# Tables moved, c spread in two rounded parts, and loads reordered in a decoder layer

## The chip, the cores and the metric

The kernel runs on one core of one Trainium2 chip, as one program. The metric is device time in microseconds, the median over several executions; lower is better. Weights are packed on the host into the order in which they are read; that is not part of the time.

## The reference

One decoder layer on 256 tokens with 2048 channels in float32. A vector c makes six modulation vectors, which shift, scale and gate two sub-layers. The first mixes tokens with block attention (eight heads; with 256 tokens there is one block of keys) and with a gated delta rule (16 value heads); the second is a SwiGLU of width 5632.

```python
mod = jax.nn.silu(c) @ w_ada[l] + b_ada[l]
sh1, sc1, g1, sh2, sc2, g2 = jnp.split(mod[:, None, :], 6, axis=-1)
h = x * (1.0 + sc1) + sh1
y = token_mixer(h, w_in[l], conv_w[l], a_log[l], dt_bias[l], gdn_norm_w[l], rel_bias,
                w_proj_moba[l], w_proj_gdn[l], w_out[l])
x = layer_norm(DEEPNORM_ALPHA * x + g1 * y, ln1_g[l], ln1_b[l])
h = x * (1.0 + sc2) + sh2
y = swiglu(h, w_ffn_in[l], w_ffn_out[l])
x = layer_norm(DEEPNORM_ALPHA * x + g2 * y, ln2_g[l], ln2_b[l])
...
proj = h @ w_in          # in token_mixer: q, k, v of both mixers, z, gates
merged = jax.nn.sigmoid(gate_a) * (y_a @ w_proj_moba) + jax.nn.sigmoid(gate_b) * (y_b @ w_proj_gdn)
return merged @ w_out
```

## The kernel before

**Products.** Every weight is loaded as float32 (`raw`, 512 KB, 128 x 1024), rounded by ScalarE into `hi` (L235), and VectorE writes the rest, raw - hi, into `lo` (L236). Activations are split in the same way. A product is hi*hi + hi*lo + lo*hi, so three matmuls of the rounded type float32r. There are three shapes of loop:

- `ws_mm` (L329 to L331): the weights are the stationary operand, 128 x 128, and 256 tokens move. h, split into s0 (high) and s1 (low), ya and ybA with ybBh/ybBl (the outputs of the two mixers) are moved in this way.
- `xs_unit` (L377 to L379): 128 tokens of the activation are stationary and 512 columns (sometimes 256) of hi or lo move. z, the output projection (activations mh, ml) and the feed-forward output (ach, acl) use it.
- `ws_wide` (L336, L340), for the feed-forward input: the high and low half of h lie side by side and move as 512 columns past hi, then 256 columns past lo.

**Stages, by the time of the profile.** Up to 17 us the opening: c is spread over 128 partitions by matmuls with a row of ones (`load_c`, L152), passed through Silu into `cb`, and `warm` (L508) issues matmuls on zeros. Up to 305 us the start: 24 jobs (256 columns of w_in each; 16 for the delta mixer, 8 for attention) times four groups of four 128-row blocks of w_in. In the first group eight of the jobs run as a *ramp*, block by block, since each block of h needs its own two modulation columns first. The partial sums of 19 jobs are added up in SBUF by VectorE, five stay in PSUM (`kept`). From 305 to about 975 us come attention, the delta rule, z, gates, branch projections and the output projection, the two mixers' steps being interleaved with the weight jobs by lanes of generators (`tick`). From 975 to 1475 us the feed-forward input, then its output and the last LayerNorm.

**Modulation columns.** One column of 128 outputs is a 1 MB load (`w_ada`, into a ring of four buffers) and one VectorE multiply-and-sum over 2048 elements with `cb` (L255, the `r<-r,cb,cols` rows). In the start 40 columns are handled this way: `ada_to(n)` makes the sums up to n, `ada_goal` says how many are due at job i of group n. `ada_opening` issues the load of column n + 3 before it makes the sum of column n, so four columns are loaded or under way. In the first group `between` puts a block of x and the two packed ramp weights behind each pair of modulation loads.

**Queues.** All of these loads are issued by SyncE in program order. A load into a buffer still in use holds the queue. `run(3)` lets the loads and splits of up to three later jobs be issued ahead of a job's matmuls; the loads and sums that a job itself issues come behind its matmuls. `prep` makes four blocks of h (two ScalarE activations and a VectorE subtraction each) near the end of the group before.

**Addresses.** Tiles of the pool `perm` lie one behind the other in the order of first use, then the weights pool, then the pool of the mixers or of the feed-forward. In the compiled program before, these are the byte addresses within a partition:

| tiles | address | modulo 128 |
|---|---|---|
| x_sb, later ya, sgb, r | 4224 | 0 |
| cb, then jk (160 bytes) | 22848, 31040 | 64, 64 |
| dtb, nwc, epsc, adac, ada_half | 31200 to 31776 | small tables |
| s0, s1 (h; later the feed-forward's h, 128 bytes on) | 32032, 48672 | 32, 32 |
| sa and other small tables | from 65312 | |
| raw, hi, lo (several buffers) | 66176, 90752, 107136 | 0, 0, 0 |
| kq, v; later mh, ml | 132736 to 157312 | 0 |
| ring of modulation columns, later ma and ybA; ybBh | 165696, 182080 | 64, 64 |
| ybBl | 206656, 214848 | 64 |
| ach, acl | 124544, 169600 | 0, 0 |

All buffers of hi, of lo and all slices that are used as operands are whole multiples of 128 bytes apart, so the last column holds for each of them.

Of the kernel before, what the change touches and what calls it, by code (L numbers as in the profile page):

```python
# [10 lines left out]
F32 = mybir.dt.float32  # L11
F32R = mybir.dt.float32r
AF = mybir.ActivationFunctionType
OP = mybir.AluOpType
# [4 lines left out]
P = 128  # L19
D = 2048  # L20
S = 256
KT = D // P
# [83 lines left out]
def layer(ctx, tc, a, out):  # L106
    nc = tc.nc
    v_, s_, g_, t_, dma = nc.vector, nc.scalar, nc.gpsimd, nc.tensor, nc.sync
    sdma = nc.gpsimd

    perm = ctx.enter_context(tc.tile_pool(name="perm", bufs=1))
    wp = ctx.enter_context(tc.tile_pool(name="wp", bufs=3))
# [12 lines left out]
    def e2(nm, shape):  # L125
        return k1.tile(shape, F32, tag="e2", name=nm, bufs=2)
# [9 lines left out]
    def load_x(k0, kn):  # L136
        dma.dma_start(x_sb[:, k0:k0 + kn, :], a["xT"][:, k0:k0 + kn, :])

    cb = perm.tile([P, D], F32, name="cb")
    jk = perm.tile([P, 40], F32, name="jk")  # L140

    def load_c():
        ones = e2("ones", [1, P])
        v_.memset(ones, 1.0)
        dma.dma_start(cb[0:1, :], a["c"])
        ps = mm()
        for i in range(3):
            t_.matmul(ps, zero[:, :P], zero, start=True, stop=True)
        for i in range(4):
            ps = (pt.tile([P, 512], F32, tag="tp", name="ps_c") if i % 2 else  # L150
                  pg.tile([P, 512], F32, tag="gd", name="ps_c"))
            t_.matmul(ps, ones, cb[0:1, 512 * i:512 * i + 512], start=True, stop=True)  # L152
            s_.activation(cb[:, 512 * i:512 * i + 512], ps, AF.Silu)  # L153

    w_in = a["w_in"]
# [95 lines left out]
    def ada_sum(col, part, raw, parts):  # L251
        first, last = part == 0, part == parts - 1
        n = D // parts
        h = ada_half[:, col % 4:col % 4 + 1]
        v_.tensor_tensor_reduce(out=raw, in0=raw, in1=cb[:, n * part:n * part + n], scale=1.0,  # L255
                                scalar=cols[:, col:col + 1] if first else h, op0=OP.mult, op1=OP.add,
                                accum_out=adac[:, col:col + 1] if last else h)
# [11 lines left out]
                ada_sum(*held.pop(0), 2)  # L269
                yield 1.35  # L270

    def ada_opening(order, ahead, between):
        held, loaded = [], 0
        for n, col in enumerate(order):
            while loaded < min(n + ahead + 1, len(order)):
                raw = ring[loaded % len(ring)]
                dma.dma_start(raw, w_ada.tile(0, KT, order[loaded] * P, P, by_column=True))
                held.append(raw)
                loaded += 1
                between(loaded)  # L280
            raw = held.pop(0)
            if n == 0:
                for half in range(2):
                    ada_sum(col, half, raw[:, 1024 * half:1024 * half + 1024], 2)
            else:
                ada_sum(col, 0, raw, 1)
            yield

    turn = {"mm": 0, "all": False}

    def mm():
# [14 lines left out]
    def do(fn):  # L306
        prog.append((None, fn, 0))
# [86 lines left out]

    hTh, hTl = [aT(tag).rearrange("p (k i) -> p k i", i=S) for tag in ("s0", "s1")]
    h_ops = [[t[:, k, :] for k in range(KT)] for t in (hTh, hTl)]

    def g8(slot, nm, shape, dt=F32):
        return k1.tile(shape, dt, tag=f"g{slot}", name=nm)
# [39 lines left out]
    RAMP = [list(range(len(jobs) - KEPT, len(jobs) - 1)), [len(jobs) - 1, 0, 1, 2]]  # L439
    raws = {}  # L440

    def between(n):
        if n % 2 or n > 2 * GROUPS[0][1]:
            return
        k = n // 2 - 1
        load_x(k, 1)
        for part, some in enumerate(RAMP):
            raw = wp.tile([P, 1024], F32, tag="raw", name="raw", bufs=6)
            dma.dma_start(raw, w_in.columns(k, [jobs[i][0] for i in some], 256))
            raws[k, part] = raw.rearrange("p (k n) -> p k n", n=256)  # L450

    ada1 = ada_opening(ada_order[:2 * KT + EARLY], 3, between)
    ada_n = [0]

    def ada_to(n):
        while ada_n[0] < n:
            next(ada1)
            ada_n[0] += 1

    def ada_goal(n, i):  # L460
        ends = [2 * (k0 + kn) for k0, kn in GROUPS] + [2 * KT + EARLY]
# [11 lines left out]
    def prep(k0, kn):  # L473
        for f in range(k0, k0 + kn):
            by = dict(bias=adac[:, f:f + 1], scale=adac[:, 16 + f:17 + f])
            s_.activation(hTh[:, f, :], x_sb[:, f, :], AF.Identity, **by)
            hf = e2("hf", [P, S])
            s_.activation(hf, x_sb[:, f, :], AF.Identity, **by)
            v_.tensor_tensor(hTl[:, f, :], hf, hTh[:, f, :].bitcast(F32), op=OP.subtract)
# [19 lines left out]

    def warm():  # L500
        ps = mm()
        two = [zero.rearrange("p (a b) -> p a b", b=b)[:, :, :b // 2] for b in (2, 32)]
        for m in [zero] * 8 + [zero[:, 0:1].to_broadcast([P, 512])] * 3 + [zero[:, :S]] * 3 + two * 2 + [zero] * 4:
            n = 512 if m is zero or m.shape[-1] == 512 else S
            o = ps[:, :n]
            if len(m.shape) == 3:
                o = o.rearrange("p (a b) -> p a b", b=m.shape[2])
            tc.keep_in_program_order(t_.matmul(o, zero[:, :P], m, start=True, stop=True))  # L508

    warm()  # L510
    kept = []
# [2 lines left out]
    def ramp(k, part):  # L514
        def post(hi, lo):
            some = RAMP[part]
            if k == 0:
                for i in some:
                    stays = i - len(jobs) + KEPT
                    if stays < 0:  # L520
                        accs[i] = mm()
                        continue
                    p, tag, b = ((pt, "tp", 2), (pt, "tp", 2), (pg, "gd", 2), (pg, "gd", 2), (pm, "mk", 1))[stays]
                    accs[i] = p.tile([P, 512], F32, tag=tag, name="mm_kept", bufs=b)
                    kept.append(accs[i])
            for low in range(2):
                for n, i in enumerate(some):
                    for t in range(2):
                        o, c = accs[i][:, t * S:(t + 1) * S], slice(t * P, (t + 1) * P)
                        if low:  # L530
                            last = k == 3 and t == 1 and i < len(jobs) - KEPT
                            t_.matmul(o, lo[:, n, c], h_ops[0][k], start=False, stop=last)
                        else:
                            t_.matmul(o, hi[:, n, c], h_ops[0][k], start=(k == 0 and t == 0), stop=False)
                            t_.matmul(o, hi[:, n, c], h_ops[1][k], start=False, stop=False)
            if part and k < 3:
                for _ in range(5):
                    t_.matmul(kept[0], zero[:, :P], zero, start=False, stop=False)
            if part and k == 3:
                for i in some[1:]:  # L540
                    s_.copy(jobs[i][1], pairs_of(accs[i]))

        held_step(lambda: raws[k, part], 4, 256, post)

    def startup(n):
        k0, kn = GROUPS[n]
        more = n + 1 < len(GROUPS)
        if n == 0:
            for k in range(4):
                do(lambda k=k: (ada_to(2 * k + 2), prep(k, 1)))  # L550
                for part in range(2):
                    ramp(k, part)
        if more:
            do(lambda: load_x(*GROUPS[n + 1]))
        if n == 1:
            do(load_small)
            do(load_ba)
        for i, (c0, dst) in enumerate(jobs):
            if n == 0 and i in RAMP[0] + RAMP[1]:
                continue  # L560

            def post(hi, lo, i=i, dst=dst):
                stays = i - len(jobs) + KEPT
                if stays < 0:
                    ps = mm()
                    ws_mm(ps, h_ops, hi, lo, k0, kn, True, True)
                else:
                    ps = kept[stays]
                    ws_mm(ps, h_ops, hi, lo, k0, kn, False, not more)
                if n == 0 if stays < 0 else not more:  # L570
                    s_.copy(dst, pairs_of(ps))
                elif stays < 0:
                    v_.tensor_tensor(dst, dst, pairs_of(ps), op=OP.add)
                ada_to(ada_goal(n, i))
                if more and i == (17 if n else 16):
                    prep(*GROUPS[n + 1])
                if not more and i >= 8:
                    if i == 8:
                        bg["pre"].append(gdn_pre(0))
                    tick()  # L580
                if not more and i == len(jobs) - 1:
                    ada_to(2 * KT + EARLY)

            step(w_in, k0, kn, c0, 256, post)
# [881 lines left out]
```

## Time and profile before

| | |
|---|---|
| median of 3 runs | 1727.77 us (1727.2 to 1731.12) |
| profiled execution | 1732.76 us, span 1731.0 us |
| TensorE busy | 97% of the span |
| VectorE, ScalarE busy | 71%, 48% |
| moved by DMA | 412.72 MB, mean 238 GB/s |

A row of the page or of the timeline names the kernel's line (L329), the engine (PE is TensorE's matmuls, PEld its weight loads, DVE VectorE, ACT ScalarE, POOL GpSimd, SP SyncE's queue of loads), the operation, the tiles as out<-in, the shape and a count. The duration of one matmul in the rows (280 to 400 ns) includes its way through the array; several overlap, so the time that a row of matmuls takes is read from the distance between their starts, or from the count in a stretch of time.

### The profile page before, as it was taken

To read this page: it belongs to the slowest core of one execution; us is meant where nothing else is said; L and a number is where in the kernel's file an instruction comes from. 1 tells how busy PE (TensorE), PEld (TensorE's weight loads), DVE (VectorE), ACT (ScalarE), POOL (GpSimd) and SP (SyncE) were. 2 spreads that over 40 slices of the span, in tenths; PEclk is the share of its full clock that TensorE was granted. 3 is DMA by queue.
4 is the path that set the end of the run, shared out by engine and by line. 5 is a ranking of instruction groups with operands and counts; after the bars stand their busy time and mean duration, and the time that the engine had idled before them with its cause. 6 is when DMAs were issued, how large, how long until landed. Compare 5 with 4: busy or idle time off the path is not lost.

```text
span 1731.0 us, 28124 instructions
## 1 busy us (share of the span) xinstructions
PE 1686.1 (97%) x11117; PEld 1509.6 (87%) x11117; DVE 1225.2 (71%) x1724; ACT 835.8 (48%) x1176; POOL 34.5 (2%) x60
## 2 busy tenths in 40 slices
PE   9999999999899998999999999999999999999997
PEld 7899999789898798889988998888888888888885
DVE  7788989786985676457989787666666666555454
ACT  3544445679554753365434454444444444433341
POOL 0000000001010000000000000000000000000000
PEclk9999999999999999899999999999999999999998
DMA  9989886576685577557999468777777776766662
GB/s 384 414 328 359 308 307 221 175 218 207 200 257 179 162 226 236 181 184 244 304 356 353 154 216 259 223 227 224 225 222 232 227 222 221 238 192 188 197 193 72
DMA packets 110582, 412.72 MB, mean 238 GB/s; under 512 B 13053, under 2 KB 14605, under 8 KB 104941
## 3 DMA queue, kind: packets, MB, share of 16 engines
q1 hardware_dynamic: 107010, 400.13, 69.7%
q0 software_dynamic: 3440, 10.80, 2.3%
q8 instruction: 87, 1.43, 0.3%
q14 instruction: 45, 0.37, 0.1%
HBM read 406.59 MB, written 4.28 MB: 237 GB/s over the span
## 4 chain that ended last, share of the span: by engine, by line
PE 78%; DVE 9%; DMA 7%; issue 3%; ACT 2%; SPq 0%; POOL 0%; DVEq 0%; ACTq 0%; POOLq 0%
PE mm L336 17%; PE mm L340 9%; PE mm L377 8%; PE mm L379 8%; PE mm L378 8%; PE mm L331 7%; PE mm L329 7%; PE mm L330 7%; DVE lo L236 4%; DMA raw_a<-in_w_ada 3%; DMA raw<-in_w_in 1%; DVE r L255 1%; DMA Mb<-mbd 1%; PE mm_kept L331 1%; PE mm_kept L329 1%
## 5 line engine op out<-in xcount | busy, mean ns | idle before, releaser
L235 ACT CAST hi<-raw 128x1024 fp32r<-128x1024 f32 x552 | 577.2, 1049 | 710.5 <-PE mm L379 199.4
L236 DVE TENSOR_TENSOR lo<-raw,hi 128x1024 fp32r<-128x1024 f32 x552 | 672.1, 1223 | 318.1 <-ACT hi L235 315.4
L331 PE MATMUL mm<-s,lo 128*128 128x256 f32 x1208 | 343.7, 285 | 12.9 <-DVE lo L236 12.9
L329 PE MATMUL mm<-s,hi 128*128 128x256 f32 x1208 | 345.2, 286 | 2.4 <-ACT hi L235 2.4
L330 PE MATMUL mm<-s,hi 128*128 128x256 f32 x1208 | 342.0, 283 | 0.0
L336 PE MATMUL mm<-s,hi 128*128 128x512 f32 x1280 | 323.7, 395 | 0.0
L336 PEld LDWEIGHTS mm<-s,hi 128*128 128x128 f32 x1280 | 229.1, 188 | 43.2
L331 PEld LDWEIGHTS mm<-s,lo 128*128 128x128 f32 x1208 | 230.2, 191 | 15.7 <-DVE lo L236 15.4
L329 PEld LDWEIGHTS mm<-s,hi 128*128 128x128 f32 x1208 | 230.0, 191 | 4.8 <-ACT hi L235 2.6
L330 PEld LDWEIGHTS mm<-s,hi 128*128 128x128 f32 x1208 | 230.1, 190 | 1.6 <-issue 1.1
L340 PEld LDWEIGHTS mm<-s,lo 128*128 128x128 f32 x1280 | 172.2, 188 | 14.7
L340 PE MATMUL mm<-s,lo 128*128 128x256 f32 x1280 | 176.0, 280 | 0.0
L377 PE MATMUL mm<-hi,ach 128*128 128x512 f32 x352 | 137.1, 390 | 0.0
L378 PE MATMUL mm<-lo,ach 128*128 128x512 f32 x352 | 137.0, 389 | 0.0
L379 PE MATMUL mm<-hi,acl 128*128 128x512 f32 x352 | 137.0, 389 | 0.0
L255 DVE CUSTOM_DVE_ANT_0 raw_a<-raw_a,cb,cols 128x1024 f32<-128x1024 f32 x56 | 71.8, 1282 | 50.0 <-DMA raw_a<-in_w_ada 50.0
L255 DVE CUSTOM_DVE_ANT_0 raw_a<-raw_a,cb,ada_half 128x1024 f32<-128x1024 f32 x56 | 71.7, 1280 | 50.0 <-DMA raw_a<-in_w_ada 49.9
L255 DVE CUSTOM_DVE_ANT_0 r<-r,cb,cols 128x2048 f32<-128x2048 f32 (+1 forms) x40 | 92.5, 2321 | 4.1 <-ACT cb L153 4.1
L377 PE MATMUL mm<-hi,s 128*128 128x512 f32 x192 | 79.4, 414 | 0.0
L378 PEld LDWEIGHTS mm<-lo,ach 128*128 128x128 f32 x352 | 66.1, 188 | 13.8
L379 PEld LDWEIGHTS mm<-hi,acl 128*128 128x128 f32 x352 | 66.1, 188 | 13.7
L377 PEld LDWEIGHTS mm<-hi,ach 128*128 128x128 f32 x352 | 66.1, 188 | 13.6
(336 smaller groups left out, 2314.0 us busy)
## 6 DMA issues: line engine op xcount, KB each, us to landing
raw<-in_w_in SPq DMA_DIRECT2D x208, 512.0 KB, 4.6
raw<-in_w_ffn_in SPq DMA_DIRECT2D x176, 512.0 KB, 4.2
raw_a<-in_w_ada SPq DMA_DIRECT2D x112, 512.0 KB, 4.4
raw<-in_w_ffn_out SPq DMA_DIRECT2D x88, 512.0 KB, 4.2
r<-in_w_ada SPq DMA_DIRECT2D x40, 1024.0 KB, 8.8
raw<-in_w_proj_gdn SPq DMA_DIRECT2D x32, 512.0 KB, 4.5
raw<-in_w_out SPq DMA_DIRECT2D x32, 512.0 KB, 6.0
raw<-in_w_proj_moba SPq DMA_DIRECT2D x16, 512.0 KB, 4.6
```

Source lines behind the costliest of these rows:

```text
L235: s_.copy(hi, raw)
L236: low = v_.tensor_tensor(lo, raw, hi.bitcast(F32), op=OP.subtract)
L255: v_.tensor_tensor_reduce(out=raw, in0=raw, in1=cb[:, n * part:n * part + n], scale=1.0, scalar=cols[:, col:col + 1] if first else h, op0= ...
L329: t_.matmul(o, hi[:, i, c], ah, start=(first and i == 0 and t == 0), stop=False)
L330: t_.matmul(o, hi[:, i, c], al, start=False, stop=False)
L331: t_.matmul(o, lo[:, i, c], ah, start=False, stop=(last and i == kn - 1 and t == 1))
L336: t_.matmul(box[t].rearrange("p (u i) -> p u i", u=2), hi[:, i, t * P:(t + 1) * P], both[k0 + i], start=(first and i == 0), stop=False)
L340: t_.matmul(box[t][:, :S], lo[:, i, t * P:(t + 1) * P], both[k0 + i][:, 0, :], start=False, stop=(last and i == kn - 1))
L377: t_.matmul(box[h], xh, hi[:, i, :], start=start, stop=False)
L378: t_.matmul(box[h], xh, lo[:, i, :], start=False, stop=False)
L379: t_.matmul(box[h], xl, hi[:, i, :], start=False, stop=stop)
```

## The change

Three things are changed. `jk`, a small table, is made after s0 and s1 instead of before them, and has 56 columns instead of 40. `load_c` rounds c into a high part and takes a rest, both float32r, and adds two products in PSUM instead of one float32 product. And the modulation loads of the start are issued by a function of its own, `ada_load`, apart from the sums: in the first group only eight columns are loaded during the ramp, and then columns are loaded up to two beyond the goal of the job (three in later groups). The load of the next group's x moves from the start of a group to its job 9. The matmuls on zeros are also fewer in `warm`, and of 256 columns in the ramp.

```diff
-    jk = perm.tile([P, 40], F32, name="jk")
 
     def load_c():
-        ones = e2("ones", [1, P])
-        v_.memset(ones, 1.0)
+        ones = k1.tile([1, P], F32R, tag="e2", name="ones", bufs=2)
+        v_.memset(ones.bitcast(F32), 1.0)
         dma.dma_start(cb[0:1, :], a["c"])
         ps = mm()
         for i in range(3):
             t_.matmul(ps, zero[:, :P], zero, start=True, stop=True)
+        parts = []
+        for i in range(4):
+            if i % 2 == 0:
+                hi = wp.tile([P, 1024], F32R, tag="hi", name="c_hi", bufs=4)
+                lo = wp.tile([P, 1088], F32R, tag="lo", name="c_lo", bufs=4)
+            part = slice(512 * (i % 2), 512 * (i % 2) + 512)
+            raw = cb[0:1, 512 * i:512 * i + 512]
+            s_.copy(hi[0:1, part], raw)
+            v_.tensor_tensor(lo[0:1, part], raw, hi[0:1, part].bitcast(F32), op=OP.subtract)
+            parts.append((hi[0:1, part], lo[0:1, part]))
         for i in range(4):
...
-            t_.matmul(ps, ones, cb[0:1, 512 * i:512 * i + 512], start=True, stop=True)
+            for n in range(2):
+                t_.matmul(ps, ones, parts[i][n], start=(n == 0), stop=(n == 1))
             s_.activation(cb[:, 512 * i:512 * i + 512], ps, AF.Silu)
...
     hTh, hTl = [aT(tag).rearrange("p (k i) -> p k i", i=S) for tag in ("s0", "s1")]
     h_ops = [[t[:, k, :] for k in range(KT)] for t in (hTh, hTl)]
+    jk = perm.tile([P, 56], F32, name="jk")
...
-    ada1 = ada_opening(ada_order[:2 * KT + EARLY], 3, between)
-    ada_n = [0]
+    early = ada_order[:2 * KT + EARLY]
+    ada_n = {"load": 0, "sum": 0, "held": []}
+
+    def ada_load(n):
+        while ada_n["load"] < min(n, len(early), ada_n["sum"] + len(ring)):
+            at = ada_n["load"]
+            raw = ring[at % len(ring)]
+            dma.dma_start(raw, w_ada.tile(0, KT, early[at] * P, P, by_column=True))
+            ada_n["held"].append(raw)
+            ada_n["load"] += 1
+            if at % 2 and at < 2 * GROUPS[0][1]:
+                k = at // 2
+                load_x(k, 1)
+                for part, some in enumerate(RAMP):
+                    raw = wp.tile([P, 1024], F32, tag="raw", name="raw", bufs=6)
+                    dma.dma_start(raw, w_in.columns(k, [jobs[i][0] for i in some], 256))
+                    raws[k, part] = raw.rearrange("p (k n) -> p k n", n=256)
 
     def ada_to(n):
-        while ada_n[0] < n:
-            next(ada1)
-            ada_n[0] += 1
+        while ada_n["sum"] < n:
+            ada_load(ada_n["sum"] + 1)
+            raw, col = ada_n["held"].pop(0), early[ada_n["sum"]]
+            if ada_n["sum"] == 0:
+                for half in range(2):
+                    ada_sum(col, half, raw[:, 1024 * half:1024 * half + 1024], 2)
+            else:
+                ada_sum(col, 0, raw, 1)
+            ada_n["sum"] += 1
...
     def warm():
         ps = mm()
-        two = [zero.rearrange("p (a b) -> p a b", b=b)[:, :, :b // 2] for b in (2, 32)]
-        for m in [zero] * 8 + [zero[:, 0:1].to_broadcast([P, 512])] * 3 + [zero[:, :S]] * 3 + two * 2 + [zero] * 4:
...
+        for _ in range(14):
+            tc.keep_in_program_order(t_.matmul(ps, zero[:, :P], zero, start=True, stop=True))
...
             if part and k < 3:
-                for _ in range(5):
-                    t_.matmul(kept[0], zero[:, :P], zero, start=False, stop=False)
+                for n in range(12):
+                    at = 16 * (2 * k + n // 6)
+                    t_.matmul(kept[0][:, :S], zero[:, 384:], zero[:, at:at + S], start=False, stop=False)
...
             for k in range(4):
-                do(lambda k=k: (ada_to(2 * k + 2), prep(k, 1)))
+                do(lambda k=k: (ada_load(min(2 * k + 4, 8)), ada_to(2 * k + 2), prep(k, 1)))
                 for part in range(2):
                     ramp(k, part)
-        if more:
-            do(lambda: load_x(*GROUPS[n + 1]))
...
-                ada_to(ada_goal(n, i))
+                goal = ada_goal(n, i)
+                ada_to(goal)
+                ada_load(goal + (3 if n else 2))
+                if more and i == 9:
+                    load_x(*GROUPS[n + 1])
                 if more and i == (17 if n else 16):
                     prep(*GROUPS[n + 1])
```

More of the change, by code (lines that the diff above doesn't have):

```diff
@@ L270, in ada_sums @@
                 yield 1.35
[L272 to L287, printed above, removed]
     turn = {"mm": 0, "all": False}
@@ L440, in layer @@
     raws = {}
[L442 to L450, printed above, removed]
-    ada1 = ada_opening(ada_order[:2 * KT + EARLY], 3, between)
-    ada_n = [0]
-    def ada_to(n):
-        while ada_n[0] < n:
-            next(ada1)
-            ada_n[0] += 1
+    early = ada_order[:2 * KT + EARLY]
[14 more added lines that the diff above has]
+                    raws[k, part] = raw.rearrange("p (k n) -> p k n", n=256)
+    def ada_to(n):
+        while ada_n["sum"] < n:
[7 more added lines that the diff above has]
+            ada_n["sum"] += 1
     def ada_goal(n, i):
@@ L501, in warm @@
         ps = mm()
-        two = [zero.rearrange("p (a b) -> p a b", b=b)[:, :, :b // 2] for b in (2, 32)]
-        for m in [zero] * 8 + [zero[:, 0:1].to_broadcast([P, 512])] * 3 + [zero[:, :S]] * 3 + two * 2 + [zero] * 4:
[L504 to L508, printed above, removed]
+        for _ in range(14):
+            tc.keep_in_program_order(t_.matmul(ps, zero[:, :P], zero, start=True, stop=True))
     warm()
```

## The prediction, before the changed kernel was run

> **What bounds the kernel now.** I read the page of the profile first, then the busy time by windows, then the timeline of the places that the diff touches, and last the chain of work that ended last.
>
> ```profile
> span 1731.0 us, 28124 instructions
> PE 1686.1 (97%) x11117; PEld 1509.6 (87%) x11117; DVE 1225.2 (71%) x1724; ACT 835.8 (48%) x1176; POOL 34.5 (2%) x60
> DMA  9989886576685577557999468777777776766662
> PE 78%; DVE 9%; DMA 7%; issue 3%; ACT 2%; SPq 0%; POOL 0%; DVEq 0%; ACTq 0%; POOLq 0%
> ```
>
> TensorE is busy for 97% of the span, so nearly all time is the number of matmuls times the distance between two starts. That distance is what the change of addresses can touch. Windows that hold one kind of matmul give it (window, length, PE busy, count, granted clock, DMA share, GB/s):
>
> ```profile
> 170.00:300.00 130.00, 130.00 (x1098) 1.00 0.82 284
> 825.00:845.00 20.00, 20.00 (x179) 1.00 0.88 300
> 960.00:970.00 10.00, 10.00 (x86) 1.00 0.60 201
> 1480.00:1700.00 220.00, 220.00 (x972) 1.00 0.62 192
> ```
>
> All four run at clock 1.00 without an idle moment. The edges cut some 2.5 matmuls, so I divide by the count less 2.5. The first three are 256 columns wide: moving s with weights hi or lo, 130/1095.5 = 118.7 ns; moving ybA or ybBh with the same weights, 20/176.5 = 113.3 ns; moving hi or lo with weights mh, 10/83.5 = 119.8 ns. The fourth is 512 wide, moving hi with weights ach: 220/970 = 226.8 ns, exactly twice 113.3. So the same instruction has three paces. The table of addresses above orders them by the distance between moving and weight address, modulo 128 bytes: 64 gives 113.3; 32 gives 118.7; 0 gives 119.8 at 256 columns but 226.8 at 512. The other 512-wide kinds both stand at 32:
>
> ```profile
> 1199.74 2.02 PE L336 MATMUL mm<-s,hi 128*128 128x512 f32 x8
> 1201.60 1.10 PE L340 MATMUL mm<-s,lo 128*128 128x256 f32 x8
> 1202.54 2.02 PE L336 MATMUL mm<-s,hi 128*128 128x512 f32 x8
> 729.83 0.39 PE L378 MATMUL mm<-lo,s 128*128 128x512 f32 x1
> 732.16 0.39 PE L379 MATMUL mm<-hi,s 128*128 128x512 f32 x1
> ```
>
> In the feed-forward input, eight wide matmuls take 1201.60-1199.74 = 1.86 us, 232.5 ns each, and eight narrow ones 0.94 us, 117.5 ns. In z, ten starts lie 2.33 us apart, 233 ns each.
>
> The start has another bound:
>
> ```profile
> 17.10:96.70 79.60, 74.73 (x592) 0.98 1.00 399
> 96.70:305.30 208.60, 206.15 (x1730) 1.00 0.85 303
> 250.00:300.00 50.00, 50.00 (x424) 50.00 (x423) 49.73 (x73) 25.42 (x33) 3.11 (x5) 1.00 0.69 225
> ```
>
> The first group of w_in rows (192 ramp matmuls, 15 fillers, 384 of the other 16 jobs, which is x592) ends at 96.7 with the DMA engines full; the three other groups (3 x 24 x 24 = 1728 matmuls) end at 305.3. In the third row (PE, PEld, DVE, ACT, POOL) VectorE is at 49.73 of 50 us.
>
> **The change, part by part.**
>
> *Addresses.* jk had 160 bytes ahead of s0 and s1; now 224 bytes stand behind them. So s0 and s1 move down by 160 and everything from sa on moves up by 64. Modulo 128: s from 32 to 0; hi, lo, raw, kq, mh, ach from 0 to 64; ma0, ybA, ybB from 64 to 0; x_sb's place, which ya has later, stays at 0. The distances become: s to hi or lo, 64 instead of 32 (all of L329 to L331, L336, L340 and z's L377 to L379 with s); ya to hi, 64 instead of 0; ybA to hi stays 64; mh and ach to hi stay 0. No instruction is added.
>
> For 256 columns the new distance is the one that ybA shows, so I take 113.3. For 512 columns no row has distance 64. The bounds are 226.8 (no penalty, as at 0) and twice 119.8, 240 (the worst narrow pace, doubled). I take 226.8: it is nearest to the narrow pace that does have distance 64, doubled, and every row with both addresses at a multiple of 64 shows either no penalty or the one of distance 0. The terms:
>
> ```profile
> L336 PE MATMUL mm<-s,hi 128*128 128x512 f32 x1280 | 323.7, 395 | 0.0
> L340 PE MATMUL mm<-s,lo 128*128 128x256 f32 x1280 | 176.0, 280 | 0.0
> 1030.00:1470.00 440.00, 440.00 (x2516) 1.00 0.73 229
> L329 PE MATMUL mm<-s,hi 128*128 128x256 f32 x624 | 180.6, 290 | 0.0
> L331 PE MATMUL mm<-s,lo 128*128 128x256 f32 x624 | 178.1, 285 | 8.8 <-DVE lo L236 8.8
> L377 PE MATMUL mm<-hi,s 128*128 128x512 f32 x192 | 79.4, 414 | 0.0
> L329 PE MATMUL mm<-ya,hi 128*128 128x256 f32 x128 | 37.5, 295 | 0.0
> ```
>
> Feed-forward input: 1280 x (232.5-226.8) + 1280 x (117.5-113.3) = 7.3 + 5.4 = 12.7 us. The third row has TensorE busy in all 440 us and DMA at 0.73, so all of it reaches the end. The middle (lines of 305 to 1030 us): 624 x 3 narrow s matmuls, of which 336 open the feed-forward; those gain 336 x 4.2 = 1.4 us. The other 1536 x 5.4 = 8.3, z's 192 x 3 x 6.2 = 3.6 and ya's 128 x 3 x 6.5 = 2.5 us make 14.4. There TensorE shares the end:
>
> ```profile
> 305.30:785.00 479.70, 350.97 (x2161) 0.98 0.66 203
> by line: PE mm L329 10.4%; PE mm L330 10.2%; PE mm L331 10.1%; PE mm L377 8.1%; PE mm L379 7.8%; PE mm L378 7.7%; DMA raw_a<-in_w_ada 6.2%; DVE lo L236 4.1%; issue 4.0%; DMA Mb<-mbd 3.1%; PE ps L838 2.4%; DMA mbd<-mc 1.3%; PE ps_ba L487 1.2
> ```
>
> The matmuls of s and ya lead 54% of the chain between 305 and 785 us; the rest waits for loads, VectorE and the attention and delta steps. I count 8 of the 14.4, a little over that share. Groups two to four: 1728 x 5.4 = 9.3 us, but in the last 50 us VectorE is full and would become the bound (424 x 5.4 = 2.3 us lost), and elsewhere it and the loads are close: 6 us.
>
> *Opening and order of loads.* These go together, since one stall ends both:
>
> ```profile
> 3.03 7.19 PE L152 MATMUL ps_c<-cb,ones 1*128 1x512 f32 x8
> 10.15 7.17 PE L508 MATMUL mm<-zero 128*128 128x512 f32 x22
> 10.26 0.60 ACT L153 ACTIVATE cb<-ps_c 128x512 f32<-128x512 f32 x1 [1.11 <-PE ps_c L152]
> 12.10 2.35 DVE L255 CUSTOM_DVE_ANT_0 r<-r,cb,cols 128x2048 f32<-128x2048 f32 x1
> 17.16 0.28 PE L534 MATMUL mm_kept<-s,hi 128*128 128x256 f32 x1
> 27.95 8.21 SPq L277 DMA_DIRECT2D r<-in_w_ada  x3
> 36.24 0.86 SPq L226 DMA_DIRECT2D raw<-in_w_in  x2
> 36.72 10.91 DMA raw<-in_w_in
> 47.53 0.39 PE L329 MATMUL mm<-s,hi 128*128 128x256 f32 x1 [2.39 <-ACT hi L235]
> 49.40 0.53 PE L331 MATMUL mm<-s,lo 128*128 128x256 f32 x1 [1.37 <-DVE lo L236]
> ```
>
> Spreading c costs eight float32 passes in 7.19 us. Now four ScalarE copies (as the 0.60 us row of 512 columns), four VectorE subtractions of 512 columns (about as long) and eight rounded matmuls run as a pipeline from the landing of c at 3.0: eight ScalarE steps of 0.6, the Silu ones behind the copies, end near 7.9 instead of 10.86. The modulation sums start 3 us sooner. Of the filling matmuls 14 of 22 remain, so they end near 13, no longer holding the ramp to 17.16. The ramp's 12 narrow fillers in place of 5 wide ones, 1.36 against 1.13 us at these paces, run while VectorE sums: nothing, or 0.7 us if that cover goes. c's halves use two of four hi and lo buffers and are free before the ramp's third step: nothing.
>
> The ramp's later steps are held by loads. Before, three 1.05 MB modulation loads stood in SyncE's queue ahead of the first ordinary weights: 27.95, then 36.24. At 399 GB/s they take 7.9 us, and the weights landed at 47.6 (36.72 + 10.91). Now those weights go first and land near 40, before the ramp ends at 43 (44.9 before). So the idle 2.39 + 1.37 us goes. Behind the moved weights now wait the modulation loads nine to eleven, whose sums are due only before the next group's h near 80 us; x for it moves to job 9, about 20 us ahead of its use. What is late next is bytes: by 87 us the group needs 12.6 MB of weights, 17 or 18 modulation columns (18.9) and 1 MB of x, 32.5 MB, where 399 GB/s since 2 us brings 33.9. On job time alone the group would end at 43 + 16 x 24 x 113.7 ns = 86.7, 10 us sooner; with that little to spare I count 8. For later groups the load depth is three columns ahead, as before: nothing.
>
> **Sum**: 12.7 + 1.4 + 8 + 6 + 8 = 36 us. The profiled execution took 1732.8 us (span 1731.0), 0.3% above the median of 1727.8; 1732.8 - 36 = 1696.7, and for the median 1691.8: **1692 us**.
>
> The Trainium skill speaks against the largest part. "SBUF — State Buffer", section "Who interferes with whom", says that only the port pair shared by VectorE and GpSimd causes contention, and its note on cachelines has lines of 16 bytes, in which distances of 0, 32 and 64 are alike. By that rule addresses are worth nothing and the sum would be the opening's 8 us alone. The windows disagree with it: 118.7, 113.3 and 119.8 ns for one shape at one clock.
>
> **The rivals.** *Only narrow matmuls gain.* At 512 columns distance 0 is good although it is bad at 256, so 64 may be bad where it is good at 256: 232.5 stays. That loses 7.3 us in the feed-forward and some 2 in z: 1701. For it speaks that reversal, against it the exact factor two. *Addresses are not the cause*: the pace follows what was written last or how busy other engines are, and a shift does nothing. Then only the opening counts, 1727.8 - 8 = 1720. Against it: mh and ybA have different paces with VectorE similarly placed, and the pace is steady for 130 us. *Slower: the new distance is the bad one at 512.* With 240 ns, 1856 wide matmuls (1280 + 576) lose 7.5 ns each, 13.9 us; if the narrow ones also go to 119.8, 7 us more, less the opening: 1727.8 + 13.9 + 7 - 8 = 1741. With the narrow ones unimproved it decides from 232.5 + 8000/1856 = 236.8 ns on; should these gain as ybA shows, even 240 ends at about 1714.
>
> **How the numbers follow.** Forecast 0.56 (own range 1682 to 1700, from all of the middle's 14 and all 10 us of the opening to half of the middle); narrow only, with wide ones unchanged or a little worse, 0.20; addresses without effect 0.12; slower 0.06; the rest, between these, 0.06. The range 1681 to 1712 leaves out the last case, most of 1720 and little else. Within 0.3% of before (5 us, what a measurement here can tell from nothing) stand few of these: faster 0.90, same 0.04, slower 0.06.
>
> **What would show it.** In the profile after: in 170 to 300 us some 1147 matmuls in place of 1098; eight L336 in 1.81 us and eight L340 in 0.91; L377 with ach at 226.8 and with mh at 119.8, unchanged. No gap of TensorE near 45 us, no half clock behind it, the first group ending by 89, the fourth near 291. The prediction is wrong if L336 stays at 232 or rises, if VectorE's lo takes the place of TensorE as what is waited for in groups two to four, or if sums wait for modulation loads before the second group.

## The result, and the profile after

| | before | after |
|---|---|---|
| median of 5 runs | 1727.57 us | 1708.04 us |
| lowest to highest | 1726.7 to 1731.12 | 1703.92 to 1716.02 |
| profiled execution, span | 1732.76, 1731.0 us | 1716.02, 1714.2 us |

The ratio is 0.9894, with a 95% interval of 0.9863 to 0.9926: faster by 1.1%, where the forecast of 1692 us said 2.1%. The time lies in the range given, not in its likeliest part (1682 to 1700). Two things stand out beside the median: the runs of the changed kernel lie 12 us apart, and the profiled one is the slowest of the five.

The page after, its first lines:

```profile
span 1714.2 us, 28148 instructions
PE 1665.8 (97%) x11130; PEld 1496.9 (87%) x11130; DVE 1225.7 (71%) x1728; ACT 839.3 (49%) x1180; POOL 34.6 (2%) x60
```

TensorE is still busy for 97% of the span, so what moved is again the distance between matmuls, and the waits. The same windows as before (window, length, TensorE busy, count, clock, DMA share, GB/s):

```profile
17.10:94.90 77.80, 71.33 (x581) 0.98 1.00 397
94.90:305.20 210.30, 205.56 (x1729) 0.99 0.85 304
170.00:300.00 130.00, 130.00 (x1106) 1.00 0.83 289
```

The first group ends at 94.9 us (96.7 before, 89 or less predicted), the fourth at 305.2 (305.3 before, 291 predicted). In 170 to 300 us there are 1106 matmuls, where 1098 stood before and 1147 were predicted: 130/1103.5 = 117.8 ns each, not 113.3. The feed-forward input, from the timeline after (start, duration, engine, line, tiles, count; L329 and L333 are now the two loops of `ws_wide`):

```profile
1184.82 0.73 PE L333 MATMUL mm<-s,lo 128*128 128x256 f32 x5
1185.38 2.00 PE L329 MATMUL mm<-s,hi 128*128 128x512 f32 x8
1187.22 1.07 PE L333 MATMUL mm<-s,lo 128*128 128x256 f32 x8
1188.13 2.00 PE L329 MATMUL mm<-s,hi 128*128 128x512 f32 x8
```

Eight wide matmuls take 1187.22 - 1185.38 = 1.84 us, 230 ns each (232.5 before, 226.8 predicted); eight narrow ones 1188.13 - 1187.22 = 0.91, 113.8 ns each (117.5 before, 113.3 predicted).

Lining up the two traces instruction by instruction from the end gives where the 16.8 us between the two profiles came from. Beside it stand three more profiles, told of below: the changed kernel a second time, the addresses alone, and the rest of the change without them.

| us won against before | predicted | after | after again | addresses alone | rest alone |
|---|---|---|---|---|---|
| up to the end of the fourth group | 14 | 0.0 | 6.4 | 6.4 | -2.6 |
| from there to the feed-forward input (1030 us) | 9.4 | 8.4 | 4.4 | 7.8 | 8.4 |
| feed-forward input | 12.7 | 8.4 | 8.4 | 8.4 | -2.1 |
| sum | 36 | 16.8 | 19.2 | 22.6 | 3.6 |

Each column compares one execution with the one profile of before. Single executions lie off their medians: the profile of before by 5 us, that of after by 8. So a sum here is not the gain of the change, which the medians give as 19.5 us.

### The profile page after: what moved, and what is told of

Its sections match the earlier page's. It is cut to its first block, busy times and chain, and to the rows that moved or that the text cites. A ratio compares the mean times of both kernels' runs of the same rounds, so it can differ in the third digit from the quotient of the medians.

```text
span 1714.2 us, 28148 instructions
## 1 busy us (share of the span) xinstructions
PE 1665.8 (97%) x11130; PEld 1496.9 (87%) x11130; DVE 1225.7 (71%) x1728; ACT 839.3 (49%) x1180; POOL 34.6 (2%) x60
## 4 chain that ended last, share of the span: by engine, by line
PE 61%; DVE 7%; DMA 5%; issue 2%; ACT 1%; DVEq 0%; ACTq 0%
PE mm L329 17%; PE mm L333 9%; PE mm L370 7%; PE mm L372 7%; PE mm L371 7%; DMA raw_a<-in_w_ada 4%; PE mm L322 4%; PE mm L323 3%; PE mm L324 3%; DVE lo L246 3%; DVE raw_a L265 1%; DMA Mb<-mbd 1%; PE ps L841 1%; ACT hi L245 0%; DMA raw<-in_w_out 0%
## 5 line engine op out<-in xcount | busy, mean ns | idle before, releaser
L322 PE MATMUL mm<-s,hi 128*128 128x256 f32 x1208 | 345.0, 286 | 2.8 <-ACT hi L245 2.6
L329 PE MATMUL mm<-s,hi 128*128 128x512 f32 x1280 | 319.6, 392 | 0.0
L329 PEld LDWEIGHTS mm<-s,hi 128*128 128x128 f32 x1280 | 228.4, 188 | 39.5
L322 PEld LDWEIGHTS mm<-s,hi 128*128 128x128 f32 x1208 | 230.7, 191 | 5.4 <-ACT hi L245 2.8
L333 PEld LDWEIGHTS mm<-s,lo 128*128 128x128 f32 x1280 | 169.9, 188 | 13.6
L333 PE MATMUL mm<-s,lo 128*128 128x256 f32 x1280 | 171.9, 277 | 0.0
```

The source lines that it names most:

```text
L322: t_.matmul(o, hi[:, i, c], ah, start=(first and i == 0 and t == 0), stop=False)
L329: t_.matmul(box[t].rearrange("p (u i) -> p u i", u=2), hi[:, i, t * P:(t + 1) * P], both[k0 + i], start=(first and i == 0), stop=False)
L333: t_.matmul(box[t][:, :S], lo[:, i, t * P:(t + 1) * P], both[k0 + i][:, 0, :], start=False, stop=(last and i == kn - 1))
```

## The experiments

The theory after the result: the pace depends on the distance between the moving and the weight address, but modulo 256 bytes and with its sign, not modulo 128; and the opening's gain is taken back because the transfers of the first two groups set their end. The rivals: the pace follows from what else runs, or from the order of loads; the first groups are held by VectorE and not by bytes. The distance is always written as moving minus weight address, modulo 256. By this count s against hi is at 160 before and at 192 after; ya against hi at 0, then 192; the feed-forward's wide matmuls at 32, then 64; its narrow ones at 160, then 192; z's, where hi moves past s, at 96, then 64.

**The two halves of the change apart.** The addresses alone are before with

```diff
-    jk = perm.tile([P, 40], F32, name="jk")
...
     h_ops = [[t[:, k, :] for k in range(KT)] for t in (hTh, hTl)]
+    jk = perm.tile([P, 56], F32, name="jk")
```

and the rest alone is after with these lines undone.

> The kernel before with jk alone moved behind s0 and s1 and made 56 wide; c, the order of loads and the fillers as before. If the addresses carry the gain and the new order of loads gives nothing in the end (theory: bytes bound the first two groups, so the 6 us of head start at 52 us is spent by 127 us), this is about as fast as the changed kernel: 1708 us, ratio 0.985 to 0.993, with the eight wide feed-forward matmuls at 1.83 us and the eight narrow ones at 0.91 us. If the order of loads carries half of the gain, it stands near 1718 (0.994). If addresses do nothing, 1727 (1.000).

> The changed kernel with jk back in its old place and 40 wide, so with the old addresses. If addresses carry the gain, 1722 to 1728 us (0.997 to 1.000); the feed-forward runs at the old 232.5 and 117.5 ns and ends with no gain of its own, and the first group is again some 6 us ahead at 52 us and nearly level at 127 us. If the order of loads carries half, 1718 (0.994).

Addresses alone: 1708.41 us (1701.78 to 1710.14), ratio 0.9875, interval 0.9856 to 0.9894. The rest alone: 1729.63 us, ratio 1.000, interval 0.9986 to 1.0014. So the whole gain comes from the addresses; c's new spread, the shorter warm-up and the new order of loads are worth nothing that can be measured. The last are not without effect: at the instruction that stood at 52 us the rest alone is 5.8 us ahead of before, at 102 us only 1.1, and between 180 and 303 us up to 2.6 behind. The gain is there and is given back. One expectation was missed: the feed-forward input of the rest alone was to be as before, and took 2.1 us more at unchanged addresses. Followed start by start, its narrow matmuls stand 118.6 ns apart where before has 117.4. The window of 170 to 300 us with the addresses alone shows what the prediction had expected of the whole:

```profile
170.00:300.00 130.00, 130.00 (x1149) 1.00 0.82 289
```

That is 130/1146.5 = 113.4 ns. Addresses of s, hi and lo are the same in this kernel and in after, where the window had 117.8. So the pace is not settled by the addresses alone.

**The pace by itself.** A kernel that computes nothing of the layer: streams of 40 matmuls on zeros, each with its own weight load, no other engine or transfer at work meanwhile; six streams for each distance, each behind a wait of TensorE of a different length.

```diff
+    for n, m0, w0 in COMBOS:
+        for r in range(6):
+            trial(n, m0, w0, (128, 160, 200, 256, 300, 350)[r])
...
+        for i in range(40):
+            w = W[:, w0 + P * (i % 8):w0 + P * (i % 8) + P]
...
+            keep(t_.matmul(o, w, x, start=True, stop=True))
```

> No layer is computed: zeros are written out, and TensorE alone runs 108 streams of 40 matmuls on zeros, for each of eight distances between moving and weight address (0, 32, ... 224 bytes; first 256 then 512 columns; then 64 the other way round) six streams, each after a wait of TensorE for VectorE of another length; other engines are idle in the streams. Theory one (the pace is drawn at each wait and then holds): at distance 64 the six streams of 256 columns show both 113.5 and 117.8 ns, at 0 only 119.8, at 32 two paces between 115 and 120. Theory two (the slower pace comes from other engines at work): every stream at distance 64 runs at 113.5. If addresses do not matter at all, all distances show the same. At 512 columns: 226.8 at 0, and at 64 226.8 or up to 232; distances that differ by 128 agree if the period is 128 bytes.

The mean distance of two starts in the last half of each stream, in ns (rounded to the value that recurs; in brackets how many of six):

| distance | 0 | 32 | 64 | 96 | 128 | 160 | 192 | 224 |
|---|---|---|---|---|---|---|---|---|
| 256 columns | 120.0 | 117.8 (3), 116.7 (3) | 117.8 | 120.0 | 118.7 | 118.7 (3), 117.3 (2), 120.0 (1) | 113.3 (3), 117.8 (3) | 118.3 to 118.5 |
| 512 columns | 226.7 | 233.3 | 229.0 | 233.3 | 231.9 (4), 232.4 (1), 233.5 (1) | 234.3 | 233.3 | 233.4 |

Three of the streams at distance 192, from the timeline of this kernel (L138 is the stream, L139 the matmul behind it):

```profile
227.00 4.93 PE L138 MATMUL ps<-M,W 128*128 128x256 f32 x40
231.77 0.22 PE L139 MATMUL ps<-G 128*128 128x128 f32 x1
232.54 4.77 PE L138 MATMUL ps<-M,W 128*128 128x256 f32 x40
237.15 0.22 PE L139 MATMUL ps<-G 128*128 128x128 f32 x1
237.98 4.93 PE L138 MATMUL ps<-M,W 128*128 128x256 f32 x40
242.74 0.23 PE L139 MATMUL ps<-G 128*128 128x128 f32 x1
```

One shape, one address pair, the rest of the core at rest, and the forty take 4.77, 4.61 and 4.76 us. Moving the weights instead of the data to make 192 gives the same two paces (113.3 five times, 117.8 once). So the distance changes the pace with TensorE on its own; neither the other engines nor the transfers are needed for it.

The table holds the steady paces of before: s 118.7 at 160, the feed-forward's wide ones 232.5 and z's 233 at 32 and 96, mh 119.8 and ach 226.8 at 0, ybA 113.3 at 192. The prediction's "64 modulo 128" had put 64 and 192 together; so had the expectation here, which looked for two paces at 64. Of the distances with more than one pace (32, 160 and 192), 192 has the two furthest apart. The trace of before shows two as well: followed start by start, s at 160 ran at 117.3 ns in most of 102 to 154 us and at 118.7 from 155 us on.

The Trainium skill, "SBUF — State Buffer", section "Who interferes with whom", gives TensorE two independent read ports, one for the moving operand and one for the weight load; these streams differ by 6% through nothing but where the two operands lie to each other.

**The changed kernel again.** Unchanged, for its profile.

> The changed kernel itself once more, for its profile alone. Theory: after each wait of TensorE the pace of the s matmuls is drawn anew, so the stretches of 113.3 and of 117.8 ns lie elsewhere than in the first profile, where 155 to 305 us was slow throughout; a start with the fast pace there ends its fourth group by 300 instead of 305 us. Rival (the pace follows from the program): the same stretches at the same places, 155 to 305 us at 117.6 ns.

It took 1713.69 us. The same window in the two profiles of the same program, first the first one, then the second:

```profile
155.00:304.00 149.00, 149.00 (x1267) 1.00 0.83 291
```

```profile
155.00:304.00 149.00, 149.00 (x1316) 1.00 0.82 294
```

117.8 and 113.4 ns, each steady over 149 us at clock 1.00. Followed matmul by matmul in these two profiles, the pace of s, ya and ybA at full clock is one of the two and changes only where the stream is broken, by a pause of TensorE or by matmuls of another kind. (With the addresses alone one change, at 83.4 us, stands at no break.) The last break in the start is near 155 us, and the pace behind it holds for 1269 matmuls, 1269 x 4.5 ns = 5.7 us. In the table above, 6.4 us of the start are there in one profile and gone in the other. With the addresses alone the fast pace held there, and in the run with distance 0 below the slow one: two of four profiles each. Not all else follows: in the middle the second profile won 4.0 us less.

**Can the better pace be forced?** First in streams: 24 matmuls at distance 192, one extra matmul of another width (at distance 0), 24 more; eight streams for each width.

```diff
+            if part == 0 and extra:
+                keep(t_.matmul(side[:, :extra], W[:, :P], M[:, :extra], start=True, stop=True))
```

> No layer is computed. Streams of 24 narrow matmuls at distance 192, then one other matmul of 0, 512, 320, 192, 128, 64 or 32 columns, then 24 narrow ones again; eight streams each, after waits of different length. If the pace is a phase that a stream keeps, the first 24 of some streams run at 113.3 and of others at 117.8; with no other matmul the second half keeps the pace of the first in all eight. If the phase is set by how a matmul ends, one length of the other matmul brings all second halves to one pace; if only a wait draws it, none does.

| width of the extra one | second half at 113.3 | at 117.8 | pace kept |
|---|---|---|---|
| none | 4 | 4 | 8 of 8 |
| 512 | 0 | 8 | 4 of 8 |
| 320 | 5 | 3 | 5 of 8 |
| 192 | 0 | 8 | 7 of 8 |
| 128 | 0 | 8 | 6 of 8 |
| 64 | 7 | 1 | 6 of 8 |
| 32 | 0 | 8 | 5 of 8 |

Without an extra matmul the pace never changes in a stream. Behind one of 64 columns the pace is mostly the fast one (five streams were fast already, and two of the three slow ones became so); it costs 142 - 113 = 29 ns. Behind 32, 128, 192 and 512 columns it was always the slow one. Then in the kernel: the second matmul of each `ws_mm` job cut in two, which leaves the products as they are, once 192 columns and then 64, once the other way round.

```diff
-                t_.matmul(o, hi[:, i, c], al, start=False, stop=False)
+                for b, e in (((0, 192), (192, S)) if i == 0 and t == 0 else ((0, S),)):
+                    t_.matmul(o[:, b:e], hi[:, i, c], al[:, b:e], start=False, stop=False)
```

> The changed kernel, in which ws_mm cuts one matmul per weight job (its second) into 192 columns and then 64; the products are the same. Theory (at distance 192 of moving and weight address there are two paces, 113.3 and 117.8 ns; a matmul of 64 columns leaves the fast one, and it stays until TensorE waits): between 155 and 305 us the 256-column matmuls stand 113.3 to 113.6 ns apart whatever the pace was after the last wait, about 1147 matmuls and some 33 cuts in 170 to 300 us where the profile of the changed kernel shows the slow pace; the start ends up to 5 us earlier than there, the middle gains 1 or 2 us, and the median is 1700 to 1706 us with runs closer together. Rival (the pace is set by something else, a loading or engine state, and the streams of zeros don't carry over): paces mixed as before, each cut costs 5 to 30 ns x about 220 jobs, 1 to 7 us, so 1709 to 1715 us.

> The same cut in the other order: 64 columns first, then 192, so the same number of instructions of the same sizes. Theory: the 192 columns come last and leave the slow pace, so the 256-column matmuls of s, ya and ybA stand 117.6 to 117.8 ns apart nearly everywhere: some 1105 in 170 to 300 us, 1728 x 4.3 = 7 us more in groups two to four and about 2000 x 4.3 x a half = 4 us more in the middle than with 192 first, so 1708 to 1718 us. Rival (order of the two parts does not matter): the same time as with 192 first within 2 us.

They took 1750.24 us (ratio 1.0141, interval 1.0118 to 1.0165) and 1749.8 (1.0135, 1.0113 to 1.0156): slower by 1.4%, alike. Both orders give 114 ns between the cuts nearly throughout 155 us to the end of the start, so the expectation that 192 columns last would leave the slow pace failed, and what an inserted matmul does in a stream can't be carried to a pair. That the cuts held the fast pace isn't shown either: it held in two of four profiles without cuts. The price was wrong too:

```profile
201.99 0.28 PE L322 MATMUL mm<-s,hi 128*128 128x256 f32 x1
202.11 0.30 PE L324 MATMUL mm<-s,hi 128*128 128x192 f32 x2
202.25 0.36 PE L325 MATMUL mm<-s,lo 128*128 128x256 f32 x1
202.45 0.28 PE L322 MATMUL mm<-s,hi 128*128 128x256 f32 x1
```

From the cut pair (the row x2) to the start of L322, 202.45 - 202.11 = 0.34 us, where two whole ones take 0.23: 0.11 us for each cut, as much as one pays for 24 slow matmuls. The 214 cuts add 23.5 us of TensorE's time. In spite of it the start was 3.4 and 3.6 us shorter than in the first profile of after; the time was lost between the start and 1030 us, 38 and 32 us against the first profile of after. The 126 cuts there make 14 us of it. The rest was not tested apart: the order of VectorE's instructions came out otherwise, and with 192 columns first modulation loads lead 30.3% of the chain between 640 and 930 us (22.9% in after). That part is no test of the pace.

**Distance 0 for the feed-forward.** The streams put 512 columns at distance 0 ahead, 226.7 against 229.0. After with h and lo of the feed-forward 64 bytes instead of 128 on, wide at 0, narrow at 192:

```diff
-        halves = [aT(tag, 32).rearrange("p (k u i) -> p k u i", u=2, i=S) for tag in ("s0", "s1")]
+        halves = [aT(tag, 16).rearrange("p (k u i) -> p k u i", u=2, i=S) for tag in ("s0", "s1")]
...
-    place["lo"] = 32
+    place["lo"] = 16
```

> The changed kernel with the feed-forward's h 64 bytes on instead of 128, and its lo too, so that wide matmuls have distance 0 to hi modulo 256 (226.7 ns in the streams) instead of 64 (229.0), and narrow ones keep 192. If the streams carry over, eight wide matmuls take 1.81 us instead of 1.83 and the feed-forward ends 2 us sooner; the total, 0.9 per mille, drowns in the spread of the changed kernel's own runs (1704 to 1716). If the period were 128, distance 0 and 64 would change the narrow ones too.

1717.13 us, ratio 0.9941, interval 0.9919 to 0.9963: less won than by after (0.9894, 0.9863 to 0.9926), though the two intervals overlap a little. From the timeline of this kernel:

```profile
1198.16 1.11 PE L333 MATMUL mm<-s,lo 128*128 128x256 f32 x8
1199.10 2.00 PE L329 MATMUL mm<-s,hi 128*128 128x512 f32 x8
1200.94 1.11 PE L333 MATMUL mm<-s,lo 128*128 128x256 f32 x8
1201.88 2.00 PE L329 MATMUL mm<-s,hi 128*128 128x512 f32 x8
```

Wide 1.84/8 = 230 ns and not 226.7; narrow 0.94/8 = 117.5, near the slow pace of 192, each time. Against before it won 3.1 us in the feed-forward input, after 8.4. The narrow ones have distance 192 in both kernels, and with the wide ones at 64 they were fast in every profile. In a loop of eight and eight the paces of unmixed streams don't hold; why isn't settled.

**Half the bytes of the start.** After with only the first half of each modulation load of the start moved. The sums still run over 2048 elements, half of them zeros, so VectorE's work is unchanged.

```diff
+    for t in ring:
+        g_.memset(t[:, 1024:], 0.0)
...
-            dma.dma_start(raw, w_ada.tile(0, KT, early[at] * P, P, by_column=True))
+            dma.dma_start(raw[:, :1024], w_ada.tile(0, KT, early[at] * P, P, by_column=True)[:, :1024])
```

> The changed kernel with half of each modulation load of the start left out (4 KB of 8 KB in each partition; the sums run over all 2048 elements as before, the other half being made of zeros at first). If bytes bound the first two groups, TensorE has no wait at 72 and none of 2 us at 98 to 111, the first group ends near 87 instead of 94.9, the second near 155 instead of 169.7, and the start is over near 290 (305). If VectorE bounds them, they end where they did, to 2 us.

1694.41 us, ratio 0.9816, interval 0.9796 to 0.9837. Its windows of the first group, and of the three others:

```profile
17.00:84.70 67.70, 66.84 (x580) 1.00 0.94 341
84.70:285.30 200.60, 200.57 (x1729) 1.00 0.76 257
```

The first group ends at 84.7 instead of 94.9 us, the others take 200.6 instead of 210.3, without an idle moment, at 200.6/1726.5 = 116.2 ns on average (113.3 up to 164 us, 117.8 behind it). So bytes set the end of the first group and the waits behind it, and VectorE, with the same sums to make, is not what held the first two groups.

None of these suggests a version that is faster than after and than the addresses alone, which are alike at 1708.

## Why the prediction came out as it did

**The largest step, that addresses set the pace, was right**, and the case against it, that addresses are worth nothing, fell: addresses alone give the whole gain, and the rest nothing. The rule for them was not: a period of 256 bytes fits all runs, and one of 128 does not. Between the medians 19.5 us were won where 36 were predicted. The time lies in the range because the range was wide enough to take in the rival with 1701, and one term of the sum was met by luck (the middle, below).

**Groups two to four, 6 us predicted: together with the opening 0 in the first profile, 6.4 in two others.** The step that failed is "for 256 columns the new distance is the one that ybA shows, so I take 113.3". The distance was right (192 for both), but ybA at 192 has two paces, and I had read only one. It stood in the trace of before, in another stretch of ybA and ybBh:

```profile
853.00:863.00 10.00, 10.00 (x87) 1.00 0.97 334
```

10/84.5 = 118.3 ns (117.8 from start to start), between two waits of TensorE, beside the 113.3 of 825 to 845 us. One window of 20 us was taken for a constant. The same step holds the second error: that VectorE, at 49.73 of 50 us, would become the bound. The second profile of after has more matmuls in the same window with less VectorE (PE, PEld, DVE, ACT, POOL):

```profile
250.00:300.00 50.00, 50.00 (x443) 49.95 (x443) 47.82 (x72) 28.06 (x38) 3.11 (x5) 1.00 0.64 215
```

**The opening, 8 us predicted: 0.** Its parts came as foreseen. The ramp begins at 12.77 instead of 17.16 us, the first ordinary job at 44.16 instead of 47.53, the first ordinary weights land at 38.4 instead of 46.4 (the prediction's 47.6 was the second load of them), and the idle 2.39 + 1.37 us and the half clock behind them are gone. At 52 us after is 6.0 us ahead. The failed step is "with that little to spare I count 8": there was nothing to spare. From the windows of after (first the ten jobs from 44.16 us, then a gap, then the other six; PE, PEld, DVE, ACT, POOL, clock, DMA share, GB/s) and its timeline:

```profile
44.16:72.60 28.44, 28.04 (x240) 27.55 (x240) 21.94 (x19) 13.34 (x19) 0.00 (x0) 1.00 1.02 414
72.60:75.40 2.80, 0.20 (x3) 0.03 (x1) 0.47 (x2) 2.58 (x5) 0.00 (x0) 1.00 0.99 408
75.40:94.90 19.50, 18.74 (x144) 18.27 (x145) 15.88 (x16) 10.91 (x16) 0.00 (x0) 0.91 0.94 346
```

```profile
75.38 0.38 PE L322 MATMUL mm<-s,hi 128*128 128x256 f32 x1 [2.60 <-ACT hi L245]
75.60 0.28 PE L323 MATMUL mm<-s,hi 128*128 128x256 f32 x1
76.64 0.38 PE L324 MATMUL mm<-s,lo 128*128 128x256 f32 x1 [0.76 <-DVE lo L246]
...
78.06 0.41 PE L323 MATMUL mm<-s,hi 128*128 128x256 f32 x1
```

The transfers were full before and are full after (414 GB/s at 1.02). Ten jobs run 3.4 us earlier, the weights of the eleventh are not there earlier, and the same stall as before comes 30 us later: 2.6 + 0.76 us, and behind it half clock (0.41 us rows, 213 ns apart, for 3.4 us). My count of bytes, 32.5 MB to be moved by 87 us where 33.9 can be, was right as a total and wrong as a test, because the queue moves loads in its order, not by what is due: up to the load that landed at 74.1 us, 28.3 MB had to pass (15 modulation loads, 8 ramp and 14 ordinary weight loads, x twice), which is 393 GB/s over 72 us. Two later waits for lo, 1.68 us at 100.0 and 1.84 at 110.3, took what was left of the lead. With half the bytes, neither the stall nor those waits came. I had listed "bytes" as what is late next, and then charged only 2 of 10 us for it.

**The feed-forward input, 12.7 us predicted: 8.4 in all three profiles of the table that have the new addresses.** Averaged over all eights of the two traces, the narrow ones went from 117.4 to 114.0 ns, 4.4 us of the 5.4 predicted. The mis-sized term is the wide one: from 232.6 to 229.4, 1280 x 3.2 ns = 4.1 us instead of 7.3. The factor "exactly twice 113.3" by which I took 226.8 for distance 64 had no row behind it; in streams 64 gives 229.0 and only 0 gives 226.7. This is the rival "only narrow matmuls gain", halfway, and its 1701 lies nearer to the result than the forecast. The 1.4 us for the narrow ones that open the feed-forward did not come: their distance went from 32 to 64, and their pace from 116.7 to 117.8 ns.

**The middle, 8 us predicted of 14.4: 8.4, 4.4 and 7.8 in three profiles.** The size was met by luck. In the first profile 6.7 of the 8.4 us arise between 428 and 453 us, where before ran 6.8 us at half clock and after did not. The rest alone, with the old addresses, won 8.4 us in the middle too, 6.0 of them in the same place. Before, then the rest alone (PE, PEld, DVE, ACT, POOL, clock, DMA share, GB/s):

```profile
428.00:453.00 25.00, 20.23 (x144) 19.76 (x143) 17.84 (x35) 14.61 (x20) 1.09 (x2) 0.86 0.69 211
428.00:453.00 25.00, 23.62 (x195) 23.16 (x194) 22.37 (x46) 16.07 (x22) 1.31 (x3) 1.00 0.81 248
```

What the addresses are worth in the middle stays open; these profiles can't tell it from what one execution does there.

The two rivals with a slower outcome or none did not occur: no distance was worse at 512 columns than the one it replaced.

## What to carry to other kernels

Before a pace from one stretch is used as a constant, look at every stretch of the same kind between two waits, and at a second execution: a value that is steady for 150 us can still be a draw. Lay the profile of a part of the change that should do nothing in a stage beside the others, too: here it showed that the gain of the middle need not come from the addresses. When a stall in a stage with full transfers is removed, count the bytes that stand in the queue ahead of the next load that is waited for, and charge its landing time; a lead of engines over a full queue is lost at the next load. And where small tables are free to move, test tile distances by streams of the very loop that is used, since unmixed streams and mixed loops had different best distances.

## What the runs showed of the hardware

The distance between two rounded matmuls with a weight load each depends on the moving minus the weight address modulo 256 bytes: 113.3 to 120.0 ns at 256 columns, 226.7 to 234.3 at 512, at clock 1.00 with nothing else running on the core. At distance 192 and 256 columns there are two steady paces, 113.3 and 117.8 ns. Which one holds is settled, with one exception seen, where the stream is broken: by a pause of TensorE, or by a single matmul of another width (one of 64 columns: fast behind it in 7 of 8). Distances 32 and 160 showed more than one pace too, closer together. No run showed what differs inside the chip between the two, nor whether the weight load is what collides, since no stream without weight loads was run.

Cutting one matmul of 256 columns into 192 and 64 cost 0.11 us, while one matmul of 64 columns added to a stream cost 0.03; what makes the difference was not tested. The transfers of the start moved 414 GB/s for 28 us at a share of 1.02, with TensorE and VectorE busy beside them.
